# A hybrid decoder step on one core: the planner's attention in four parts, a new DMA price, and filler products where the plan leaves TensorE idle

## The chip, the core and the metric

The kernel runs on one core of a Trainium2 chip. The time is the device time of one execution in microseconds; of the kernel before there are three runs. One more execution was taken with the hardware profiler, and its rows are what this document reads.

## The reference

One inference step of a one-layer decoder in float32, for 512 prompt tokens and 8 sequences of 8 new tokens (64 sample tokens), so 576 columns in all. Every token goes through one combined input projection `w_in`; three branches read it, and their gated, normalized outputs go through `w_out`:

- a state-space branch (S5), with a scan over the tokens;
- latent attention (MLA): 8 heads; the query has a part of 128 and a rotary part of 64. `q = rmsnorm(concat(q_nope, rope(q_rot)))`, keys and values come from a latent of 256, the prompt attends causally over itself, each sample token over 1024 paged positions and the new ones;
- cross attention of 4 heads over 256 memory tokens, for prompt and sample.

```python
o = concat([rmsnorm(y_ssm) * silu(g_ssm), rmsnorm(y_mla) * silu(g_mla), rmsnorm(y_mem) * silu(g_mem)])
return x + o @ w_out
```

## The kernel before, in words

Activations stand transposed in SBUF: 128 features by 576 tokens, taken as two halves of 288 columns. Every float32 operand is split into a rounded high part and the rest (`split`, line 815), and a product is three TensorE products of those parts (`mm3`, line 845). Weights come in units of 128x512 (`wunit`, line 850): a load on SP's queue, then the high part on ScalarE or VectorE, then the low part on VectorE or, for the parts named in `ADDED` (line 32), by a DMA on GpSimd's queue that adds.

The order of the work isn't that of the code. `record` (line 2104) runs through the whole computation once and writes down every operation with the part that it belongs to: `x`, `u`, `e`, `q`, `gates0` to `gates3`, `memkv`, `mla` (attention of the prompt), `samp` (attention of the sample), `mems` (memory attention of the sample), `out` and so on. Then:

- `arrange` (line 369) gives every operation a key. A table, `ROWS` (line 41), has a row for each group of parts with two fractions of the plan's whole TensorE time, and a part's operations are spread between the two; no key is smaller than that of an operation that is waited for. From the keys come due times.
- `schedule` (line 428) plays the five engines through with costs of its own, and takes for each engine that is free the ready operation that is due first. An operation may be ahead of the oldest unfinished one by at most `self.window` (line 310; 57.7 us for TensorE, 40.7 us for SP). It also places the tiles in SBUF and in the eight PSUM banks. Prices of TensorE are by columns (line 720), with a model of the clock's two levels (`Clock`, line 265). A load on SP's queue costs 0.53 us of SP (line 601), and lands after 0.65 us, its bytes at 355e3 bytes a us, and 0.7 us more (lines 602 and 603).
- `emit` (line 648) issues the instructions in the order that came out. Each engine works through its own in that order, and waits on semaphores where an operand or a buffer isn't there yet.

The operations near the change:

- `consts` (line 921) sets `ones` (128x128) and a tile of zeros (128x288), and issues 16 products of the two (`WARM`) before the first real ones. The zeros' tile is free again after that.
- `mla_prompt` (line 1606) splits the query latent, and works in two halves of four heads. Each half begins with `mla_rot` (line 1444): 48 products for the rotary parts, the rotation on VectorE and GpSimd, and then 16 loads on SP's queue that move 32 rows each into another order (line 1469). `mla_group` (line 1477) follows twice, for two heads each: query products, sums of squares, key products with another round of norms (a row of them goes out to HBM and comes back spread over all partitions), values, and `mla_head` with its softmax.
- `mla_sample_q` (line 1620) begins with the query norms of all eight heads, so that `samp` can begin only when the last group of `mla` has its norms. `mems` needs nothing of `mla`.
- `out_proj` (line 2059) is the last product, 16 tiles of 96 products.

Of the kernel before, what the change touches and what calls it, by code (L numbers as in the profile page):

```python
# [18 lines left out]
P = 128  # L19
NT = 576  # L20
HF = 288
# [7 lines left out]
AFTER = ("mla", "samp")  # L29
SUMMED = (0, 1)  # L30
WHOLE = ("mla",)
ADDED = ("mla", "mems")
# [9 lines left out]
    (["x", "c", "u", "xn", "u3"], 0.0260741, 0.0604397),  # L42
    (["params"], 0.0288371, 0.0594688),
    (["e"], 0.054421, 0.13581),
    (["memkv"], 0.0589691, 0.14307),
    (["qm"], 0.113623, 0.153941),
    (["gates1"], 0.140543, 0.3),
    (["gates0"], 0.162105, 0.34697),
    (["scan"], 0.0965253, 0.273106),
    (["ssm", "glu"], 0.296516, 0.401341),  # L50
    (["memq", "memh"], 0.0899708, 0.278225),
    (["q", "kv", "kr"], 0.19873, 0.351389),
    (["gates2"], 0.322613, 0.380623),
    (["gates3"], 0.348796, 0.384288),
    (["mla"], 0.408448, 0.505007),
    (["samp"], 0.469029, 0.791363),
    (["mems"], 0.60639, 0.775131),
    (["fin0", "fin1", "fin2", "fins"], 0.649241, 0.728233),
    (["out"], 0.796155, 0.986057),
# [205 lines left out]
class Clock:  # L265
# [3 lines left out]
    def __init__(self):  # L269
        self.work, self.state, self.last = {}, {-1: 1.0, 0: 1.0}, 0  # L270
# [19 lines left out]
class Plan:  # L290


    def __init__(self, F, R, PS, sizes, place):
        self.F, self.R, self.PSt, self.sizes, self.place = F, R, PS, sizes, place
        self.ops = []
        self.tiles = []
        self.part = ""
        self.parts = {}
        self.lead = 0.0
        self.trace = None  # L300
        self.soon = 19.2555
        self.edf = True
        self.margin = [0, 0, 730, 0, 0, 0, 0]
        self.steal = 0.2575
        self.look, self.stall, self.tol = 15, 175.4667, 5.0000
        self.late = False
        self.hide = 0.6578
        self.early = 0.07
        self.slack = 1.0
        self.window = [57.6874, 40.6910, 40.6910, 40.6910, 40.0202]  # L310
# [58 lines left out]
    def arrange(self, rows):  # L369
# [21 lines left out]
        for o in reversed(self.ops):  # L391
            d = max(o.forms[o.eng][1], o.weights)
            if o.eng == SP:
                d = 2.5 + d / 355e3
            elif o.info == "dma_start":
                d = 5.9
            took[o.pos] = d
            k = key[o.pos]
            x = k if o.eng == PE else k + self.soon
            for s in o.succ:  # L400
                x = min(x, due[s.pos] - d - latency(o.eng, s.eng))
            due[o.pos] = x
# [25 lines left out]
    def schedule(self):  # L428
# [49 lines left out]
        dma_free = 0.0  # L478
# [13 lines left out]
        while len(order) < n:  # L492
# [18 lines left out]
            for e in range(5):  # L511
# [73 lines left out]
                for it in look:  # L585
                    heapq.heappush(h, it)
                if got is None:
# [12 lines left out]
                if e == SP:  # L600
                    avail[e] = now + (1.13 if op.info == "page" else 0.53)
                    dma_free = max(dma_free, avail[e] + 0.65) + dur / 355e3
                    op.end = dma_free + 0.7
                else:
# [5 lines left out]
                    if e == PE:  # L610
                        dur = clock.run(op.start, dur)
                    op.end = op.start + dur
# [152 lines left out]
class Hymba:  # L765
# [155 lines left out]
    def consts(self):  # L921
# [6 lines left out]
        self.G.memset(z.bitcast(F32), 0.0)  # L928
        for _ in range(WARM):
            self.mm(ps[:, :HF], self.ones, z, True, True)  # L930

# [674 lines left out]
    def mla_prompt(self):  # L1606
# [7 lines left out]
        for g in range(2):  # L1614
            qr, sq = self.mla_rot(g)
            for i in range(2):
                self.mla_group(2 * g + i, qr, sq)
# [460 lines left out]
    def run(self):  # L2078
        nc = self.nc
        with self.tc.tile_pool(name="sb", bufs=1) as sb, self.tc.tile_pool(name="pp", bufs=1, space=PSUM) as pp, \  # L2080
# [17 lines left out]
            self.record()  # L2098
            plan.arrange(ROWS)
# [74 lines left out]


# [12 lines left out]
```

## Time and profile before

| | before |
|---|---|
| median of 3 runs | 1185.97 us (1184.35 to 1188.2) |
| the profiled execution | 1190.08 us, span 1188.3 us |
| busy TensorE products | 1150.2 us, 97% of the span |
| busy VectorE | 849.0 us, 71% |
| busy ScalarE | 562.7 us, 47% |
| granted TensorE clock, mean | 0.993 |
| chain that ended last | TensorE 74%, VectorE 13%, DMA 7%, ScalarE 3% |

The span runs from the first instruction to the last one; 1.8 us of the profiled execution lie around it. A busy TensorE isn't yet one at its peak, since the ends of products are modelled: where two rows have the same busy time, their counts of products tell them apart. A granted clock of 1.00 is the higher of two levels, 2.4 GHz, and 0.50 the lower, 1.2 GHz.

### The profile page before, as it was taken

Reading aid. Unit: us, or ns where it says so; the run is one execution under the profiler, and the core shown is the slowest. Engines: PE = TensorE matmul, PEld = TensorE weight load, DVE = VectorE, ACT = ScalarE, POOL = GpSimd, SP = SyncE. Lnnn points to the kernel's source line nnn. Section 1 sums busy time; section 2 is a strip of 40 time slices with the busy share of each in tenths; the row PEclk is TensorE's granted clock in tenths of the full one; section 3 lists DMA queues with packets and bytes.
Section 4 is the critical chain, followed back from the end, with each engine's and each line's share of the span. In section 5 each row is a group of like instructions: output and inputs, shape, how many; then the busy total and the mean of one; then the engine's idle time right before and its main releaser. Section 6 shows DMA issues by size and latency. Waiting matters only on the chain.

```text
span 1188.3 us, 24276 instructions
## 1 busy us (share of the span) xinstructions
PE 1150.2 (97%) x8428; PEld 1097.8 (92%) x8428; DVE 849.0 (71%) x2252; ACT 562.7 (47%) x1712; POOL 201.3 (17%) x356
## 2 busy tenths in 40 slices
PE   8999999999999999998898999999999999999998
PEld 8989998999999999998786888899898899999998
DVE  7999599985697865457887987778999975322210
ACT  7446234431224433244764566666798863311200
POOL 1121012000114421012131210123453300000000
PEclk9999999999999999999998999999999998999999
DMA  9276211332313224467573331458778844634410
GB/s 328 91 213 213 73 62 58 125 130 78 118 45 101 94 75 149 147 192 178 148 196 97 89 94 43 120 156 206 203 186 242 213 140 132 201 111 132 146 48 30
DMA packets 98509, 160.51 MB, mean 135 GB/s; under 512 B 11378, under 2 KB 37362, under 8 KB 98386
## 3 DMA queue, kind: packets, MB, share of 16 engines
q1 hardware_dynamic: 90898, 145.33, 38.6%
q0 software_dynamic: 7488, 13.63, 6.5%
q8 instruction: 66, 1.08, 0.4%
q14 instruction: 57, 0.47, 0.1%
HBM read 125.20 MB, written 17.73 MB: 120 GB/s over the span
## 4 chain that ended last, share of the span: by engine, by line
PE 74%; DVE 13%; DMA 7%; ACT 3%; issue 2%; SPq 1%; POOL 0%; ACTq 0%; DVEq 0%
PE PS L680 72%; DVE t L680 9%; DVE F L680 4%; ACT t L680 3%; DMA t<-in_w_in 2%; PE PS L679 1%; DMA t<-re 1%; DMA t<-t 1%; SPq L680 1%; DMA t<-in_pages 1%; DMA t<-in_w_uk 1%; DMA t<-in_memT 0%; DMA t<-in_w_ukT 0%; ACT F L680 0%; DMA t<-in_cmv 0%
## 5 line engine op out<-in xcount | busy, mean ns | idle before, releaser
L680 PE MATMUL PS<-t,t 128*128 128x288 f32 (+7 forms) x8076 | 1133.1, 300 | 25.5 <-ACT t L680 17.5
L680 PEld LDWEIGHTS PS<-t,t 128*128 128x128 f32 (+2 forms) x8076 | 1067.8, 186 | 66.8 <-ACT t L680 22.0
L680 ACT ACTIVATE t<-t 128x512 fp32r<-128x512 f32 (+7 forms) x495 | 293.1, 620 | 375.3 <-DVE t L680 111.2
L680 DVE TENSOR_TENSOR t<-t,t 128x512 fp32r<-128x512 f32 (+12 forms) x616 | 354.2, 598 | 110.3 <-ACT t L680 62.5
L680 DVE TENSOR_TENSOR t<-PS,t 128x288 f32<-128x288 f32 (+5 forms) x226 | 90.9, 429 | 109.5 <-PE PS L680 105.0
L680 ACT ACTIVATE t<-PS 128x256 f32<-128x256 f32 (+7 forms) x246 | 86.6, 389 | 75.9 <-PE PS L680 43.2
L680 ACT ACTIVATE F<-PS 128x128 f32<-128x128 f32 (+1 forms) x264 | 71.4, 292 | 28.3 <-PE PS L680 25.0
L680 POOL TENSOR_TENSOR t<-t,t 128x384 fp32r<-128x384 f32 (+10 forms) x49 | 53.5, 1099 | 174.0 <-DVE t L680 119.4
L680 DVE TENSOR_SCALAR t<-t 128x512 fp32r<-128x512 f32 (+7 forms) x151 | 61.6, 419 | 29.2 <-PE PS L680 6.1
L680 POOL DMA_DIRECT2D t<-t x52 | 46.9, 908 | 150.6 <-ACT t L680 84.5
L680 DVE TENSOR_REDUCE F<-t 128x4 f32<-128x512 f32 (+1 forms) x73 | 51.7, 726 | 17.7 <-ACT t L680 17.5
L677 POOL MEMSET t<- 128x4 f32 (+2 forms) x100 | 33.5, 368 | 145.8 <-PE PS L680 107.7
L680 ACT ACTIVATE t<-t,F 128x576 fp32r<-128x576 f32 (+6 forms) x76 | 47.0, 632 | 20.0 <-DMA t<-t 11.9
L680 DVE SCALAR_TENSOR_TENSOR t<-t,t 128x576 f32<-128x576 f32 (+1 forms) x68 | 52.2, 769 | 4.6 <-ACT t L680 4.3
L680 ACT ACTIVATION_READ_ACCUMULATOR F<-PS 128x1 f32 x256 | 55.4, 219 | 0.0
L680 DVE SCALAR_TENSOR_TENSOR t<-t,F,t 128x576 fp32r<-128x576 f32 (+5 forms) x68 | 49.5, 735 | 8.1 <-ACT t L680 5.2
L680 ACT COPY t<-PS 128x64 f32<-128x64 f32 (+8 forms) x167 | 39.7, 287 | 23.2 <-PE PS L680 23.1
L680 DVE SCALAR_TENSOR_TENSOR F<-F 128x64 f32<-128x64 f32 (+5 forms) x157 | 35.1, 229 | 2.0 <-ACT F L680 0.6
L680 ACT ACTIVATE F<-F 128x256 f32<-128x256 f32 (+5 forms) x56 | 24.4, 435 | 21.8 <-DVE F L680 21.7
L680 DVE TENSOR_SCALAR t<-PS 128x256 fp32r<-128x256 f32 (+7 forms) x68 | 27.3, 408 | 9.8 <-PE PS L679 4.5
L679 PE MATMUL PS<-t,t 128*128 128x128 f32 (+1 forms) x152 | 29.6, 270 | 2.5 <-ACT t L680 1.7
L680 ACT ACTIVATE t<-PS,F 128x256 f32<-128x256 f32 (+4 forms) x39 | 18.5, 495 | 20.9 <-DVE F L680 9.6
(79 smaller groups left out, 425.5 us busy)
## 6 DMA issues: line engine op xcount, KB each, us to landing
t<-in_w_in SPq DMA_DIRECT2D x124, 256.0 KB, 3.2
t<-in_w_out SPq DMA_DIRECT2D x64, 256.0 KB, 4.6
t<-in_pages SPq DMA_DIRECT2D x64, 224.0 KB, 3.2
t<-t POOLq DMA_DIRECT2D x52, 256.0 KB, 4.4
t<-in_xT SPq DMA_DIRECT2D x32, 288.0 KB, 5.4
t<-re SPq DMA_DIRECT2D x32, 256.0 KB, 4.3
t<-in_pages SPq DMA_DIRECT2D x64, 128.0 KB, 2.3
re<-t SPq DMA_DIRECT2D x24, 256.0 KB, 2.1
```

What stands on the lines that cost most here:

```text
L677: return real(r["out"], r["value"])
L679: return real(r["out"], r["in_"], r["identity"])
L680: return real(**r)
```

## The change

It does six things.

1. The part `mla` is cut in five: `mla` keeps the latent's split and the loads of cosines and sines, `rot0` and `rot1` are the two calls of `mla_rot`, `mla0` and `mla1` the groups of the two halves. `rot1` gets a row of its own, ahead of the others.
2. All rows of the table get new numbers.
3. The planner prices loads anew, and lets at most eight be in flight.
4. Where TensorE finds no operation in the plan for more than `idle` = 0.5 us and a bank is free, `schedule` puts in a product of `ones` and zeros (128x128 by 128x288) into that bank, and goes on so until a real operation can start.
5. So that the zeros' tile lives to the end, a last product of `ones` and zeros stands at the end of `out`.
6. Some constants of the planner are rounded; `stall`, its weight for a weight load that isn't done, goes from 175 to 119.

```diff
-AFTER = ("mla", "samp")
+AFTER = ("mla0", "mla1", "samp")
-WHOLE = ("mla",)
-ADDED = ("mla", "mems")
+WHOLE = ("rot0", "rot1", "mla0", "mla1")
+ADDED = ("mla", "rot0", "rot1", "mla0", "mla1", "mems")
...
-    (["gates2"], 0.322613, 0.380623),
-    (["gates3"], 0.348796, 0.384288),
-    (["mla"], 0.408448, 0.505007),
-    (["samp"], 0.469029, 0.791363),
-    (["mems"], 0.60639, 0.775131),
-    (["fin0", "fin1", "fin2", "fins"], 0.649241, 0.728233),
-    (["out"], 0.796155, 0.986057),
+    (["gates2"], 0.3239, 0.4028),
+    (["gates3"], 0.3464, 0.3882),
+    (["rot1"], 0.3909, 0.3979),
+    (["mla", "rot0", "mla0", "mla1"], 0.4149, 0.5198),
+    (["samp"], 0.5183, 0.7914),
+    (["mems"], 0.5517, 0.7204),
+    (["fin0", "fin1", "fin2", "fins"], 0.6163, 0.729),
+    (["out"], 0.8, 1),
...
-        self.look, self.stall, self.tol = 15, 175.4667, 5.0000
+        self.look, self.stall, self.tol = 15, 119.4500, 5.0000
         self.late = False
+        self.filler, self.idle = None, 0.5
...
             if o.eng == SP:
-                d = 2.5 + d / 355e3
+                d = 3.3 + d / 400e3
...
+                if got is None and e == PE and self.filler and now > clock.busy + self.idle and order and free[BANKS] and front < n:
+
+                    op = self.filler(free[BANKS][-1][0])
+                    op.start, op.eng, op.dur = now, PE, clock.run(now, op.forms[PE][1])
+                    op.end = avail[PE] = now + op.dur
+                    order.append(op)
+                    progressed = True
+                    continue
...
                 if e == SP:
-                    avail[e] = now + (1.13 if op.info == "page" else 0.53)
-                    dma_free = max(dma_free, avail[e] + 0.65) + dur / 355e3
-                    op.end = dma_free + 0.7
+                    avail[e] = now + (1.13 if op.info == "page" else 0.5)
+                    dma_free = max(dma_free, avail[e] + 0.85) + dur / 400e3
+                    op.end = dma_free + 1.0
+
+                    flight.append(op.end)
+                    if len(flight) >= 8:
+                        avail[e] = max(avail[e], flight[-8])
...
                     if e == PE:
                         dur = clock.run(op.start, dur)
+                        clock.busy = op.start + dur
...
         for g in range(2):
+            self.plan.part = f"rot{g}"
             qr, sq = self.mla_rot(g)
+            self.plan.part = f"mla{g}"
             for i in range(2):
                 self.mla_group(2 * g + i, qr, sq)
...
         self.out_proj()
 
+        self.mm(self.bank()[:, :HF], self.ones, self.zero, True, True)
```

The function `filler` builds the product of `ones` and `self.zero` for a bank's address, without any operation that it waits for or that waits for it in the plan. The rows of the table that are left out change in the third or fourth decimal, with two exceptions: `params` begins at 0.0406 in place of 0.0288 and ends at 0.0666 in place of 0.0595, and `scan` ends at 0.2631 in place of 0.2731.

## Rows read from the trace of the kernel before

**Rows 1.** The page: span, products of TensorE, granted clock in 40 slices.

```profile
span 1188.3 us, 24276 instructions
...
PE 1150.2 (97%) x8428; PEld 1097.8 (92%) x8428; DVE 849.0 (71%) x2252; ACT 562.7 (47%) x1712; POOL 201.3 (17%) x356
...
PEclk9999999999999999999998999999999998999999
```

**Rows 2.** Windows of 30 us: busy time (count) by engine, granted clock, DMA share, GB/s.

```profile
540.00:570.00 30.00, 25.52 (x176) 22.58 (x175) 20.72 (x53) 14.81 (x35) 6.70 (x8) 1.00 0.71 164
570.00:600.00 30.00, 27.69 (x200) 24.87 (x198) 25.72 (x101) 20.97 (x56) 6.14 (x8) 1.00 0.64 166
600.00:630.00 30.00, 26.18 (x193) 23.91 (x192) 26.76 (x101) 20.81 (x53) 9.63 (x10) 1.00 0.59 166
630.00:660.00 30.00, 26.17 (x153) 22.42 (x152) 22.25 (x70) 12.09 (x31) 4.32 (x6) 0.83 0.55 146
...
690.00:720.00 30.00, 28.94 (x213) 26.98 (x213) 25.69 (x100) 16.64 (x72) 2.98 (x10) 1.00 0.22 67
...
1050.00:1080.00 30.00, 30.00 (x227) 30.00 (x227) 7.56 (x14) 6.38 (x11) 0.00 (x0) 1.00 0.39 122
```

**Rows 3.** Timeline of TensorE's products in the first 16 us: start, length, idle before.

```profile
1.27 4.21 PE L680 MATMUL PS<-R 128*128 128x288 f32 x16 [1.27 <-POOL R L677]
5.28 0.82 PE L680 MATMUL PS<-t,t 128*128 128x288 f32 x2
9.24 7.05 PE L680 MATMUL PS<-t,t 128*128 128x288 f32 x34 [3.14 <-ACT t L680]
```

**Rows 4.** Windows within the first 21 us, as in rows 2.

```profile
9.30:14.30 5.00, 5.00 (x21) 5.00 (x22) 5.00 (x9) 4.96 (x9) 0.00 (x0) 1.00 1.05 397
16.00:21.00 5.00, 5.00 (x40) 5.00 (x39) 5.00 (x9) 5.00 (x9) 0.00 (x0) 1.00 1.02 383
```

**Rows 5.** The chain that ended last, from 642 to 652 us.

```profile
642.63 3.46 DMA t<-t
...
646.21 0.96 DVE t L680 x2
...
647.96 3.90 PE PS L680 x14
```

**Rows 6.** Timeline of SP's loads in the prompt's attention; t<-t are the rotary ones.

```profile
555.30 12.22 SPq L680 DMA_DIRECT2D t<-t  x16
...
569.22 1.29 SPq L680 DMA_DIRECT2D t<-re  x3
...
638.25 4.97 SPq L680 DMA_DIRECT2D t<-t  x8
...
643.95 4.59 SPq L680 DMA_DIRECT2D t<-t  x6
```

**Rows 7.** Windows around the first fall of the clock, as in rows 2.

```profile
642.70:646.10 3.40, 1.60 (x11) 1.22 (x11) 0.92 (x2) 0.58 (x2) 0.18 (x1) 0.95 0.48 144
646.10:649.50 3.40, 1.54 (x3) 0.75 (x4) 3.11 (x7) 2.10 (x6) 0.00 (x0) 0.50 0.50 124
649.50:653.00 3.50, 3.50 (x20) 3.42 (x19) 1.69 (x5) 1.70 (x5) 0.00 (x0) 0.50 0.54 141
653.00:656.00 3.00, 3.00 (x12) 2.71 (x11) 1.72 (x8) 1.15 (x2) 0.88 (x1) 0.50 0.89 257
```

**Rows 8.** Windows around the second fall of the clock, as in rows 2.

```profile
986.40:990.50 4.10, 4.10 (x39) 4.09 (x37) 0.96 (x3) 0.02 (x1) 0.00 (x0) 1.00 0.85 268
990.50:997.30 6.80, 6.80 (x32) 6.66 (x31) 3.09 (x5) 2.68 (x6) 0.00 (x0) 0.50 0.24 72
997.30:1004.10 6.80, 6.80 (x53) 6.80 (x53) 4.31 (x21) 3.50 (x12) 0.00 (x0) 1.00 0.00 0
```

**Rows 9.** DMA issues: tensor, queue, count, KB each, median us to landing.

```profile
t<-in_w_in SPq DMA_DIRECT2D x124, 256.0 KB, 3.2
...
t<-re SPq DMA_DIRECT2D x32, 256.0 KB, 4.3
```

**Rows 10.** Waits of TensorE: us in total, times, longest.

```profile
PE PS L680 <- ACT t L680: 17.5, 13, 3.5
```

**Rows 11.** Timeline of TensorE: the first product that needs all heads' query norms.

```profile
684.29 1.12 PE L680 MATMUL PS<-t,R 64*128 64x512 f32 x2
```

More of the change, by code (lines that the diff above doesn't have):

```diff
@@ L41 @@
 ROWS = [[
[L42 to L52, printed above, removed]
-    (["gates2"], 0.322613, 0.380623),
-    (["gates3"], 0.348796, 0.384288),
-    (["mla"], 0.408448, 0.505007),
-    (["samp"], 0.469029, 0.791363),
-    (["mems"], 0.60639, 0.775131),
-    (["fin0", "fin1", "fin2", "fins"], 0.649241, 0.728233),
-    (["out"], 0.796155, 0.986057),
+    (["x", "c", "u", "xn", "u3"], 0.0262, 0.0602),
+    (["params"], 0.0406, 0.0666),
+    (["e"], 0.0556, 0.1349),
+    (["memkv"], 0.0573, 0.1431),
+    (["qm"], 0.1186, 0.1564),
+    (["gates1"], 0.1405, 0.3),
+    (["gates0"], 0.1591, 0.347),
+    (["scan"], 0.0927, 0.2631),
+    (["ssm", "glu"], 0.2928, 0.4021),
+    (["memq", "memh"], 0.09, 0.2678),
+    (["q", "kv", "kr"], 0.1967, 0.3521),
+    (["gates2"], 0.3239, 0.4028),
[6 more added lines that the diff above has]
+    (["out"], 0.8, 1),
 ]]
@@ L269, in __init__ @@
     def __init__(self):
-        self.work, self.state, self.last = {}, {-1: 1.0, 0: 1.0}, 0
+        self.work, self.state, self.last, self.busy = {}, {-1: 1.0, 0: 1.0}, 0, 0.0
     def at(self, t):
@@ L300, in __init__ @@
         self.trace = None
-        self.soon = 19.2555
+        self.soon = 19.2600
         self.edf = True
         self.margin = [0, 0, 730, 0, 0, 0, 0]
-        self.steal = 0.2575
-        self.look, self.stall, self.tol = 15, 175.4667, 5.0000
+        self.steal = 0.2600
+        self.look, self.stall, self.tol = 15, 119.4500, 5.0000
         self.late = False
-        self.hide = 0.6578
+        self.filler, self.idle = None, 0.5
+        self.hide = 0.6600
         self.early = 0.07
         self.slack = 1.0
-        self.window = [57.6874, 40.6910, 40.6910, 40.6910, 40.0202]
+        self.window = [57.6900, 40.6900, 40.6900, 40.6900, 40.0200]
     def sb(self, n, dt=F32, rows=P):
@@ L477, in schedule @@
         backfree, onfree = 0.0, False
-        dma_free = 0.0
+        dma_free, flight = 0.0, []
         clock = Clock()
@@ L491, in schedule @@
         now = 0.0
-        while len(order) < n:
+        while front < n:
             while releases and releases[0][0] <= now + 1e-9:
@@ L928, in consts, with filler @@
         self.G.memset(z.bitcast(F32), 0.0)
+        self.zero = z
         for _ in range(WARM):
             self.mm(ps[:, :HF], self.ones, z, True, True)
+    def filler(self, addr):
+        t = Tile_(512, BANKS)
+        t.addr = addr
+        ps = View(t, bass.AP(tensor=self.plan.PSt.tensor, offset=0, ap=[[self.plan.PSt.ap[0][0], P], [1, HF]]))
+        kw = dict(out=ps, lhsT=self.ones, rhs=self.zero, start=True, stop=True)
+        op = Op()
+        op.eng, op.forms, op.info, op.part, op.tiles, op.pred, op.succ = PE, {PE: self.T.form("matmul", kw)}, "filler", "filler", [], [], []
+        op.weights, op.half, op.key, op.done = 0.0, False, 0.0, True
+        return op
     def consts2(self):
@@ L2098, in run @@
             self.record()
+            plan.filler = self.filler
             plan.arrange(ROWS)
```

## The prediction

> **What bounds the kernel now.** First the page's line of engines: TensorE's products are busy for 1150.2 of 1188.3 us, and no other engine comes near [rows 1]. So the time is TensorE's products, plus 38.1 us in which none runs, plus what the products lose at the lower clock. The line of the granted clock shows two slices below 9; everything else is at 2.4 GHz. Then the windows of 30 us tell where the rest lies. The last stage runs 227 products per window with no idle time, which is the density to compare with. The prompt's attention has 176, 200, 193 and 153 products in its four windows, and 4.48, 2.31, 3.82 and 3.83 us of idle time, 14.4 in all, while VectorE is busy for at most 26.76 of 30 us and ScalarE for at most 20.97 [rows 2]. No engine is full there: the stage waits on chains of short steps. The change can gain in four places: the start, the attention's idle time, and the two falls of the clock.
>
> **1. The start.** The 16 constant products are over at 5.28 us, two real ones follow, then 3.14 us of nothing until a load's split is done [rows 3]. From 9.30 to 14.30 us TensorE makes 21 products of 288 columns in 5.00 us, 238 ns each; from 16 to 21 us it makes 40, with those cut by the edges [rows 4]. The clock's column says 1.00 in both, but a product of 288 columns in 238 ns is the 1.2 GHz level: the record of the clock isn't there yet, and the counts decide. The engine had stood idle before. Fillers go into just such a hole, since the plan too has to wait for the first loads there. If they keep the engine busy from 5.28 to 9.24 us, the 21 products may come at the higher clock: 21 x (238 - 132) = 2.2 us, with 132 ns from the 227 products per 30 us [rows 2]. The data keep up: x tiles and weights are split by VectorE and ScalarE, full in that window but for the same work that later feeds 40 products per 5 us [rows 4]. Bounds: 0 if the clock rises no earlier; -3.1 if the hole itself shrinks too, which fillers can't do. I take -2.3, counting the product that straddles the end.
>
> **2. The second half's rotary part, moved ahead.** At 644.5 us TensorE stops for 3.5 us. The chain that ended last names the cause: a rotary load lands after 3.46 us, two VectorE steps follow, and only then do the sums of squares at 647.96 go on [rows 5]. VectorE works in order, and behind its step on the late load stand the steps that those sums need. The load is late because 16 of its kind sit on SP's queue from 638.25 us on, 0.62 us of the queue each in the first eight and 0.77 in the next six [rows 6]. The pause then costs a second time: the clock falls at once, and the three windows after it are at 0.50 with 1.54 + 3.50 + 3.00 = 8.04 us of busy time [rows 7], half of which, 4.0 us, the higher clock would save. With `rot1` ahead of the first group, those 16 loads are long done by then. Bound of the gain: 3.5 + 4.0 = 7.5 us. What is late next: `rot0`'s own 16 loads held SP for 12.22 us, with the read-back of the key norms queued behind them until 569.22 [rows 6]; 16 more at that place take as long again. The cover is `rot1`'s 48 products, 48 x 0.132 = 6.3 us, and the gates that now end later. So 12.2 - 6.3 = 5.9 us could come back at worst; I take 1.5, since only the group's own loads stand behind the queue and the planner may now put them ahead of `rot1`'s. Term: -7.5 + 1.5 = -6.0, between -7.5 and -1.6.
>
> **3. The other rows and the price of loads.** The rest of the attention's idle time is 14.4 - 3.5 = 10.9 us [rows 2]. A better order could regain all of it, a worse one add as much; these are the bounds. A load of 256 KB (262144 bytes) was priced at 0.53 + 0.65 + 0.74 + 0.70 = 2.62 us and is now 0.50 + 0.85 + 0.66 + 1.00 = 3.01; the rows say 3.2 for weights and 4.3 for the read-back [rows 9]. So the new price closes 0.39 of a gap of 1.68 us, a quarter, for the load that is furthest off; a quarter of 10.9 is 2.5, and only some of these waits are for loads. I take -1.0. The Trainium skill ("DMA: Bandwidth & Descriptors", "Anatomy of one DMA", for descriptors written by software) gives 2.0 us and the bytes at 436e3 a us, 2.6 us by estimate, and by it the old price was right and this term is nothing; the rows above disagree with it, and I go by them.
>
> **4. The second fall, at 990.5 us.** It comes without any idle time: 4.10 of 4.10 us busy before it, 32 products in 6.80 us in it, 53 in the 6.80 after [rows 8]. Fillers go only where the plan finds no operation, and here it found one each time. 0, with a bound of -3.4 (half of 6.80) should the new order break up the small products.
>
> **5. What fillers cost.** Fillers stand in TensorE's own order; a real product that is ready earlier than planned stands behind them. TensorE waited 13 times for ScalarE's tiles, 17.5 us in all [rows 10]; a filler too many at each is 13 x 0.132 = 1.7 us, and none at all is 0. I take 1.0. A filler also waits for its bank's last reader on ScalarE or VectorE; the next real product mostly waits for the same engine, so nothing is added. The product at the end adds 0.13, and the zeros' 128x288 in SBUF nothing as long as plans fit.
>
> **Sum:** -2.3 - 6.0 - 1.0 + 0 + 1.0 + 0.1 = -8.2 us. The profiled execution took 1190.08 us, 4.1 more than the median: 1181.9 beside 1190.1, so 1177.8 beside 1185.97. I say 1178.
>
> **Rivals.**
> - *The wait moves and doesn't go.* The SP queue is as long as before, only earlier, and what `rot0` and `rot1` hold up at the attention's head is worth what was gained at 644 us (5.9 back, and a pause that lowers the clock there as it did here). For it: 12.22 us of queue, already with a read-back behind [rows 6]. Against it: the gates still have products at that place. Then only the start is left: -2.3 + 1.1, about 1185.
> - *Slower: the sample's attention comes too late to fill in.* From 684.29 us on, its products are mixed with the last groups' [rows 11], and there the idle time is 1.06 us per 30, against 3.8 before [rows 2]. The change moves `samp` from 0.469 to 0.518, 57 us on TensorE's 1150.2 [rows 1]. If its loads and splits are asked for so much later that the attention's last 45 us run alone, that costs 45/30 x (3.8 - 1.1) = 4.1 us, and one more pause that drops the clock, 4.0; with no gain from term 2, since the second half is then bound by its own chains: -2.3 + 8.1 + 1.1 = +6.9, 1193. It decides once the sample's first product comes later than the attention's last. Against it: those first products need the last group's norms in either plan.
> - *Fillers overrun.* The plan counts 0.13 us for one, but 16 constants took 5.28 - 1.27 us at the start, 0.25 each [rows 3]: there they last twice as long as planned. From 16 fillers on they reach past 9.24 us. With 27 (a planned hole of 4 us less 0.5) the first real products are 27 x 0.25 - 3.5 = 3.3 us late, which outweighs the gain of 2.3; with two fillers too many at 13 waits, 3.4, and no gain elsewhere, +4 to +5 before the new order's gains, some +2.5 with a part of them: 1188.5. The Trainium skill ("TensorE: Matmul & The Clock Gate", "Step-by-step: what each phase is for") says that TensorE keeps its products in program order and pulls only weight loads ahead, so nothing would overtake a filler; no row of before can show that.
>
> **How the numbers follow.** The forecast has 0.52; the wait that moves 0.18; the late sample 0.22; the overrun 0.08. The order of the whole kernel is drawn anew, and the idle time of the attention can go either way, hence the 0.22. A measurement of this kernel can tell about 0.3%, 3.6 us, from no change. The forecast's own range is 1168 to 1182.4, all faster; the second and fourth case are within 0.3%; the third is slower. Range: 1167 to 1195, which leaves out the tail of term 3's bound and the worst of the late sample.
>
> **What would show it.** Right: 21 early products at 132 ns; SP's 32 rotary loads in one block before the first group's, and none near the second half; no clock of 0.50 in the attention; 190 products or more in each window of 30 us there; the fall near the end still there. Wrong: idle time at the attention's head as long as the 3.5 us that left; a stretch after the attention's last product before the sample's first; fillers directly ahead of products whose operands had long been there.

## The result, and the profile after

The changed kernel takes 1174.74 us (median of 4 runs, 1174.41 to 1177.06) where the kernel before took 1187.09 in the same rounds (4 runs, 1184.35 to 1189.17): a ratio of 0.9899 [0.9875, 0.9924], 12.4 us faster. The forecast was 1178, 8 us faster, with a range of 1167 to 1195. So direction and range hold, and a third of the gain was not foreseen. Most of what follows is about which step it came from, since the total came out for other reasons than the sum's.

| | before | after |
|---|---|---|
| the profiled execution | 1190.08 us, span 1188.3 | 1177.06 us, span 1175.3 |
| busy TensorE products | 1150.2 us | 1150.7 us |
| span less that | 38.1 us | 24.6 us |
| granted clock, mean | 0.993 | 0.992 |

First the page of the changed kernel: span, engines and granted clock in 40 slices.

```profile
span 1175.3 us, 24339 instructions
...
PE 1150.7 (98%) x8463; PEld 1099.9 (94%) x8463; DVE 848.5 (72%) x2242; ACT 562.4 (48%) x1722; POOL 198.4 (17%) x356
...
PEclk9999999999999999999999999999999998999999
```

Against [rows 1], TensorE has 35 more products, and its busy time is the same; the span is 13.0 us shorter, and time without a product fell by 13.5. The mean clock has not risen. So in these two profiles the gain shows as time without a product. The 35 added products last some 5 us by estimate (eleven push the first real one from 5.28 to 7.51 us, 24 more take 0.13 each), so the others must have become shorter by about as much, in part at the start (below). Where the idle time lay, the windows of 30 us tell for the attention (columns as in [rows 2]):

```profile
540.00:570.00 30.00, 25.43 (x178) 22.91 (x177) 23.48 (x56) 17.03 (x40) 7.98 (x10) 1.00 0.65 167
570.00:600.00 30.00, 28.89 (x208) 25.78 (x207) 26.23 (x101) 20.81 (x59) 4.66 (x7) 1.00 0.49 126
600.00:630.00 30.00, 29.22 (x209) 25.55 (x208) 24.91 (x102) 18.86 (x51) 4.24 (x6) 1.00 0.45 110
630.00:660.00 30.00, 29.43 (x211) 26.06 (x209) 25.14 (x100) 19.19 (x56) 4.79 (x6) 1.00 0.42 120
690.00:720.00 30.00, 29.00 (x188) 27.09 (x187) 22.68 (x67) 19.10 (x88) 10.02 (x28) 0.89 0.58 146
```

The attention's four windows have 4.57, 1.11, 0.78 and 0.57 us of idle time, 7.0 in all where there were 14.4, and 806 products where there were 722. That is 7.4 of the 13.5 us. The clock no longer falls there. It falls elsewhere, at 690 to 720 us, where [rows 2] had 213 products and 1.00.

The start, as TensorE's timeline (start, length, idle before):

```profile
1.28 6.40 PE L695 MATMUL PS<-R 128*128 128x288 f32 x27 [1.28 <-POOL R L692]
7.51 0.42 PE L695 MATMUL PS<-t,t 128*128 128x288 f32 x2
```

and as a window with the columns of [rows 4]:

```profile
9.30:14.30 5.00, 5.00 (x39) 5.00 (x39) 4.76 (x8) 5.00 (x10) 0.00 (x0) 1.00 1.04 388
```

Eleven fillers stand behind the 16 constants, and are over at 7.51 us, before the data are there (0.95 us of idle time remain, where [rows 3] had 3.14: 2.2 more of the 13.5). From 9.30 to 14.30 us TensorE makes 39 products in place of 21 [rows 4].

SP's rotary loads, and what TensorE waited for on ScalarE in the whole span (us in total, times, longest):

```profile
548.11 17.48 SPq L695 DMA_DIRECT2D t<-t  x24
...
566.27 4.95 SPq L695 DMA_DIRECT2D t<-t  x8
```

```profile
PE PS L695 <- ACT t L695: 5.0, 9, 1.7
...
PE PS L694 <- ACT t L695: 2.8, 4, 1.6
```

All 32 loads are issued from 548 to 571 us, and none near the second half. [Rows 6] had 16 at 555 and the other 16 from 638 on. The row of [rows 10] shrank from 17.5 us in 13 waits to 5.0 in 9; the second row above, of another line of the kernel, is not in [rows 10] and had 2.0 us in 4 before.

Last the clock, in windows with columns as in [rows 7], around the two falls that this profile has:

```profile
693.00:699.90 6.90, 6.58 (x58) 6.40 (x57) 6.82 (x15) 2.84 (x15) 2.01 (x10) 1.00 0.32 111
699.90:706.70 6.80, 6.12 (x23) 5.48 (x22) 5.32 (x31) 5.60 (x25) 4.04 (x14) 0.50 0.61 171
...
970.00:976.40 6.40, 6.40 (x59) 6.40 (x57) 1.99 (x5) 0.86 (x3) 0.00 (x0) 1.00 0.81 258
976.40:986.60 10.20, 10.02 (x43) 9.68 (x43) 4.85 (x14) 2.92 (x8) 0.00 (x0) 0.50 0.01 2
986.60:996.80 10.20, 10.20 (x78) 10.20 (x77) 6.66 (x21) 4.62 (x13) 0.00 (x0) 1.00 0.36 106
```

The fall at 645.8 us [rows 7] is gone, a new one of 6.8 us has come at 699.9, and the one near the end [rows 8] now lasts 10.2 us in place of 6.8. The recorded time at 1.2 GHz is the same 17.0 us, in other places. The record of the clock begins where the clock first rises, at 14.3 us before and at 7.0 us after; what lies ahead of that counts as full speed.

### The profile page after: what moved, and what is told of

Same layout as the page of the kernel before. It is cut to its first block, busy times and chain, and to the rows that moved or that the text cites. A ratio compares the mean times of both kernels' runs of the same rounds, so it can differ in the third digit from the quotient of the medians.

```text
span 1175.3 us, 24339 instructions
## 1 busy us (share of the span) xinstructions
PE 1150.7 (98%) x8463; PEld 1099.9 (94%) x8463; DVE 848.5 (72%) x2242; ACT 562.4 (48%) x1722; POOL 198.4 (17%) x356
## 4 chain that ended last, share of the span: by engine, by line
PE 49%; DVE 5%; ACT 3%; DMA 2%; SPq 2%; issue 1%; POOL 0%; ACTq 0%; DVEq 0%; POOLq 0%
PE PS L695 49%; DVE t L695 3%; ACT t L695 2%; DVE F L695 2%; DMA t<-in_pages 1%; SPq L695 1%; DMA t<-in_w_uv 1%; PE PS L694 1%; SPq L1708 0%; ACT F L695 0%; DMA t<-in_w_uk 0%; SPq L1709 0%; DMA re<-t 0%; DVE PS L695 0%; POOL t L695 0%
## 5 line engine op out<-in xcount | busy, mean ns | idle before, releaser
L695 PE MATMUL PS<-t,t 128*128 128x288 f32 (+9 forms) x8076 | 1126.1, 299 | 9.9 <-ACT t L695 5.0
L695 ACT ACTIVATE t<-t 128x512 fp32r<-128x512 f32 (+7 forms) x486 | 286.5, 620 | 374.7 <-PE PS L695 121.4
L695 DVE TENSOR_TENSOR t<-t,t 128x512 fp32r<-128x512 f32 (+12 forms) x620 | 361.9, 607 | 125.8 <-ACT t L695 67.1
L695 DVE TENSOR_TENSOR t<-PS,t 128x288 f32<-128x288 f32 (+6 forms) x226 | 89.8, 428 | 89.8 <-PE PS L695 82.6
L695 ACT ACTIVATE t<-PS 128x256 f32<-128x256 f32 (+6 forms) x253 | 87.7, 392 | 66.2 <-PE PS L695 32.6
L695 POOL TENSOR_TENSOR t<-t,t 128x256 f32<-128x256 f32 (+10 forms) x45 | 41.4, 929 | 192.0 <-DVE t L695 72.7
L695 ACT ACTIVATE t<-t,F 128x576 fp32r<-128x576 f32 (+6 forms) x80 | 49.5, 633 | 14.4 <-DMA t<-t 8.2
L694 PE MATMUL PS<-t,t 128*128 128x128 f32 (+1 forms) x152 | 26.1, 269 | 5.8 <-ACT t L695 2.8
L695 DVE TENSOR_SCALAR t<-PS 128x256 fp32r<-128x256 f32 (+8 forms) x61 | 24.0, 403 | 9.9 <-PE PS L695 5.4
L695 POOL TENSOR_SCALAR t<-t 64x64 f32<-64x64 f32 (+4 forms) x24 | 21.9, 911 | 33.3 <-DVE t L695 32.0
```

The costliest lines, as they stand in the source:

```text
L694: return real(r["out"], r["in_"], r["identity"])
L695: return real(**r)
```

## The experiments

Twelve runs, four at a time; each four ran on one chip and share the runs of the kernel before. "Clock" is the mean of the granted clock over the runs of a kernel. "At full clock" is the median times that clock. It is an estimate of what would be left if all that the lower clock costs were given back; it holds as far as TensorE bounds the kernel, and is only used to tell a gain in order from a gain in clock. Since a low start counts as full in some executions and not in others, differences of 0.001 to 0.002 in the clock tell little. A ratio is taken to the runs of before on the same chip, whose median went from 1184.18 to 1187.97 us, so between chips medians and ratios can differ.

| kernel | median us | ratio to before | clock | at full clock |
|---|---|---|---|---|
| before (first four) | 1184.18 | | 0.9915 | 1174.2 |
| new order, no fillers | 1181.96 | 1.0002 [0.9973, 1.0031] | 0.9874 | 1167.1 |
| new order, fillers at the start only | 1180.59 | 0.9973 [0.9949, 0.9997] | 0.9874 | 1165.7 |
| changed, `rot1` back | 1177.53 | 0.9954 [0.9929, 0.998] | 0.9939 | 1170.4 |
| before, `rot1` ahead | 1182.54 | 0.9999 [0.9973, 1.0024] | 0.9908 | 1171.6 |
| before (second four) | 1185.85 | | 0.9905 | 1174.6 |
| changed | 1176.67 | 0.9921 [0.9895, 0.9947] | 0.9912 | 1166.3 |
| before, with fillers | 1185.63 | 0.9996 [0.9972, 1.0019] | 0.9899 | 1173.7 |
| before, ten more constants | 1187.14 | 1.0002 [0.998, 1.0025] | 0.9886 | 1173.6 |
| changed, constants among products of 64 columns | 1175.43 | 0.9917 [0.989, 0.9944] | 0.9977 | 1172.7 |
| before (third four) | 1187.97 | | 0.9899 | 1176.0 |
| new order, no fillers (again) | 1184.41 | 0.9981 [0.9965, 0.9997] | 0.9860 | 1167.8 |
| new order, late fillers only | 1179.20 | 0.9936 [0.9913, 0.9959] | 0.9895 | 1166.8 |
| changed, fewer such constants, and some in `e` | 1179.40 | 0.9941 [0.992, 0.9961] | 0.9932 | 1171.3 |
| changed | 1175.81 | 0.9908 [0.9889, 0.9928] | 0.9908 | 1165.0 |

The changed kernel was timed three times in all: 0.9899, 0.9921, 0.9908. Single runs of the kernel before went from 1177.1 to 1192.5 us, and so small differences are read with care.

### The order without its fillers

The same order of instructions to the letter, with all 34 fillers left out; run twice.

```diff
         for op in self.order:
+            if op.info == "filler":
+                continue
```

> The changed kernel's order to the letter, with its 34 planned fillers left out as the instructions are issued (the last constant product at the end stays). Nothing depends on a filler, so only their own time and the clock change. Theory A (fillers are worth the start alone): the clock is low until about 14 us again, 21 products at 238 ns, +2.5 us; the 22 fillers near 404 and 872 us stand directly ahead of products that go on without a pause, and leaving them out gives back up to 1.5 + 1.4 = 2.9 us. Sum 1174 to 1177, no change beyond 0.3%. Theory C (fillers hold the clock later too): new stretches at 0.50 near 404 and 872 us, each of 7 to 10 us, 3.4 to 5 us each: 1180 or more.

Measured: 1.0002 [0.9973, 1.0031]. And again on another chip:

> The changed kernel's order without its planned fillers once more, now on the same chip as the changed kernel. Theory D (order and fillers only help together): 0.997 to 1.002 of the kernel before, as the first time, with the changed kernel near 0.991. Theory E (the new order is the gain and the first measure of this kernel was a chip's own): 0.992 to 0.996.

Measured: 0.9981 [0.9965, 0.9997], where the changed kernel beside it had 0.9908 [0.9889, 0.9928]. **Without its fillers the new order is worth 0 to 0.2%.** That isn't for want of a better order: the span less the busy products is 31.4 us in the second profile (1181.7 - 1150.3) against 38.1 before, and at full clock the two runs give 1167.1 and 1167.8, 7 to 8 us below their own before. But the mean clock is 0.9874 and 0.9860, some 0.004 lower than before's, which is 5 us. What the order gained, the clock took back. The profile of the second run shows one of the places, where ten fillers and two more would stand. TensorE's timeline of it:

```profile
405.89 0.79 PE L697 MATMUL PS<-t,t 128*128 128x288 f32 x4 [0.46 <-ACT t L697]
408.08 1.33 PE L697 MATMUL PS<-t,t 128*128 128x288 f32 x4 [1.40 <-DVE t L697]
```

Its windows (the 400.00 one holds the pauses, the next one the clock behind them):

```profile
400.00:407.90 7.90, 6.03 (x43) 5.28 (x42) 7.87 (x15) 3.69 (x8) 5.06 (x7) 1.00 0.49 160
407.90:411.30 3.40, 3.22 (x30) 3.15 (x31) 2.93 (x6) 0.00 (x0) 0.00 (x0) 0.50 0.00 0
```

And the changed kernel at the same place, TensorE's timeline (PS<-R are the fillers):

```profile
403.91 0.43 PE L695 MATMUL PS<-R 128*128 128x288 f32 x2
404.53 0.80 PE L695 MATMUL PS<-t,t 128*128 128x288 f32 x4 [0.19 <-ACT t L695]
405.17 1.48 PE L695 MATMUL PS<-R 128*128 128x288 f32 x10
406.73 1.10 PE L695 MATMUL PS<-t,t 128*128 128x288 f32 x8
```

and its windows:

```profile
400.00:407.90 7.90, 7.63 (x62) 7.08 (x61) 7.80 (x16) 2.34 (x6) 3.80 (x5) 1.00 0.44 141
407.90:411.30 3.40, 3.40 (x57) 3.40 (x55) 2.82 (x8) 0.63 (x1) 0.53 (x1) 1.00 0.17 57
```

Where the fillers are left out TensorE idles for 0.46 and 1.40 us, and the clock falls right behind; where they stand, 57 products pass in those 3.40 us in place of 30. Set side by side by the number of the real product, the kernel without loses 1.4 us from 404 to 411 us. It isn't so in each execution: the profile of the first run has the same two pauses (0.46 and 1.37 us) and no fall behind them, and loses nothing there.

```profile
407.90:411.30 3.40, 3.40 (x60) 3.40 (x59) 2.85 (x7) 0.63 (x1) 0.53 (x1) 1.00 0.12 39
```

That profile has a fall of 3.4 us at 875.9 instead, right behind a pause of 1.64 us where the other ten late fillers would stand. The second run's has one more at 568, where no filler stands in either kernel:

```profile
568.30:571.70 3.40, 2.77 (x8) 1.90 (x9) 2.84 (x7) 2.42 (x7) 0.00 (x0) 0.51 0.62 167
```

Of the three profiles of this order without the late fillers (these two, and the one with fillers at the start only) two have falls near 407 and 568 us and one near 876; none of the six profiles of this order with them has any of the three.

### Which fillers

The 11 at the start alone, and the 23 later ones alone, by the time that the plan gives them:

```diff
+            if op.info == "filler" and op.start > 10.0:
+                continue
```

> The changed kernel's order to the letter, with only the 11 fillers of the first 10 us issued. Theory A: the clock is up at 7 us as in the changed kernel, the 22 later fillers were pure cost, so 1.5 to 2.9 us less than the changed kernel: about 1172. Theory C: the clock falls near 404 or 872 us: 1178 or more.

Measured: 0.9973 [0.9949, 0.9997], with the clock at 0.9874 as without any filler.

```diff
+            if op.info == "filler" and op.start < 10.0:
+                continue
```

> The changed kernel's order, with the 22 fillers near 404 and 872 us and the last product, but without the 11 at the start. Theory D with the gain at the start: 0.996 to 0.999 of before. With the gain in the later ones (the clock held at 404 and 872 us, some 1.5 us each, as the falls of the two kernels without them suggest): 0.993 to 0.996. Between the two, each place has its share.

Measured: 0.9936 [0.9913, 0.9959], beside 0.9981 [0.9965, 0.9997] with none and 0.9908 [0.9889, 0.9928] with all on the same chip. **The late fillers are worth 0.45%**, 5.2 us, and the intervals don't overlap; the same comparison with those at the start in place, 0.9973 against the changed kernel's 0.9899 to 0.9921, says 0.5 to 0.7%, across chips. The clock went from 0.9860 to 0.9895, 4.1 us of the 5.2. The direct saving at 404 us is 1.4 of the 5.2 in the profile that has the fall there; the rest is spread over other places, and isn't the same in two profiles. The start's fillers are worth 0.29% both times (1.0002 to 0.9973, 0.9936 to 0.9908), but both pairs of intervals overlap, so that is less sure.

### The fillers on the order of before

The planner of before with the fillers alone (28 of them, and the last product; table, parts and prices untouched):

```diff
+                if got is None and e == PE and self.filler and now > clock.busy + self.idle and order and free[BANKS] and front < n:
+                    op = self.filler(free[BANKS][-1][0])
...
+        self.mm(self.bank()[:, :HF], self.ones, self.zero, True, True)
```

> The kernel before, with its own table, parts and prices, and the fillers of the change (with the last constant product): 28 fillers, 10 of them at the start and the others late in the sample's attention. Theory A (fillers are worth the start): -2.3 + 1, 0.998 to 1.000 of before. Theory C (fillers are most of the change's gain): 0.990 to 0.994.

Measured: 0.9996 [0.9972, 1.0019]. Nothing, though the span less the busy products fell to 29.1 us (1183.7 - 1154.6), and the start had 40 products in 9.30 to 14.30 us there too. Its later fillers stand near 761, 893 and 928 us, where the profile of before has no fall of the clock, and a fall near 645 and one near 987 us are still in its own. And the start by itself, ten more constants behind the 16:

```diff
+            if op.eng == PE and op.part == "x":
+                warm += 1
+                if warm == WARM:
+                    for _ in range(10):
+                        op.forms[PE][0]()
```

> The kernel before, its order to the letter, with ten more constant products issued directly behind the 16 that open it, and nothing else. It measures the start alone. Theory A: clock up before 9.3 us, 21 products at 132 in place of 238 ns, 2.2 us, 0.998 of before. Theory C: the same; the rest of its gain would then have to be in the later fillers.

Measured: 1.0002 [0.998, 1.0025]. Its windows at the start and at 70 us:

```profile
9.30:14.30 5.00, 5.00 (x40) 5.00 (x39) 5.00 (x9) 4.99 (x9) 0.00 (x0) 1.00 1.02 382
...
70.00:74.00 4.00, 1.64 (x9) 1.09 (x8) 3.94 (x11) 2.69 (x5) 0.78 (x1) 0.99 0.91 250
74.00:84.20 10.20, 9.95 (x48) 9.82 (x48) 8.28 (x24) 5.25 (x21) 4.35 (x8) 0.50 0.51 165
```

The same windows of the kernel before:

```profile
70.00:74.00 4.00, 4.00 (x26) 3.49 (x24) 4.00 (x21) 0.44 (x1) 0.00 (x0) 1.00 0.93 267
74.00:84.20 10.20, 7.90 (x58) 6.61 (x56) 9.59 (x29) 6.87 (x26) 2.94 (x5) 1.00 0.69 203
```

From 50 to 70 us this kernel is 4.3 us ahead, product by product. At 70 us TensorE is busy for 1.64 of 4.00 us, waiting for what isn't there yet, and the clock falls for 10.2 us. At 90 us it is 0.3 us ahead. **In this profile what the start gained was given back at the next place where the data were late**, by way of the clock. The profile of before with fillers has no fall there, and its time didn't drop either, so this is one way and not the only one.

### The rotary part of the second half

The changed kernel with `rot1` back between the halves, planned anew (24 fillers):

```diff
-    (["rot1"], 0.3909, 0.3979),
-    (["mla", "rot0", "mla0", "mla1"], 0.4149, 0.5198),
+    (["mla", "rot0", "mla0", "rot1", "mla1"], 0.4149, 0.5198),
```

> The changed kernel with the row of rot1 taken away and rot1 put back between mla0 and mla1 in their own row; fillers, prices and all other rows stay. The plan is drawn anew from the attention on. Theory A (rot1 ahead is worth some 6 us): a pause of 2 to 4 us with SP's queue full of rotary loads before the second half, perhaps with a fall of the clock: 1179 to 1182. Theory B (rows and prices did it, rot1 is nothing): 1173 to 1177.

Measured: 0.9954 [0.9929, 0.998]. SP's rotary loads of the second half in its timeline:

```profile
630.30 8.67 SPq L694 DMA_DIRECT2D t<-t  x13
```

TensorE's timeline, the first products behind the rotary part:

```profile
638.81 2.24 PE L694 MATMUL PS<-t,t 128*72 128x384 f32 x12 [0.73 <-ACT t L694]
```

And the sum over the attention's four windows, from 540 to 660 us:

```profile
sum 120.00, PE 112.94 PEld 98.47 DVE 98.99 ACT 72.41 POOL 21.79; mean PE 28.24 PEld 24.62 DVE 24.75 ACT 18.10 POOL 5.45
```

The pause of 3.5 us is 0.73 here, and the idle time of the attention is 120 - 112.94 = 7.1 us, as in the changed kernel with `rot1` ahead. So what else changed in the planner, numbers and prices, takes the pause away without the move.

The move alone, on the table of before (parts cut in five, no new prices, no fillers):

```diff
-    (["mla"], 0.408448, 0.505007),
+    (["rot1"], 0.3909, 0.3979),
+    (["mla", "rot0", "mla0", "mla1"], 0.408448, 0.505007),
```

> The kernel before with the parts cut as in the change and rot1 in a row of its own ahead of the attention; the attention's other rows, the prices and everything else are those of before, no fillers. Theory A: the pause at 644 us and the fall of the clock behind it are gone, 6 to 7.5 us less than before, 1179.5 to 1181. Theory B: within 3 us of before, since what rot1 gains is lost where the 32 rotary loads now stand on SP's queue.

Measured: 0.9999 [0.9973, 1.0024]. SP's timeline at the attention's head:

```profile
547.02 23.74 SPq L681 DMA_DIRECT2D t<-t  x32
```

TensorE's timeline there:

```profile
566.17 5.92 PE L681 MATMUL PS<-t,t 128*72 128x384 f32 x33 [4.93 <-ACT t L681]
```

And the window behind the pause:

```profile
566.20:569.60 3.40, 3.40 (x11) 2.62 (x12) 2.85 (x10) 1.76 (x5) 0.00 (x0) 0.53 0.46 114
```

Much of the rival "the wait moves and doesn't go" is here: all 32 loads in one block of 23.74 us, a pause of 4.93 us at the head in place of 3.5 in the middle, and the clock falls behind it there (11 products in 3.40 us). But the head had a pause before the move too, of 2.27 us,

```profile
565.54 2.29 PE L680 MATMUL PS<-t,t 128*72 128x384 f32 x12 [2.27 <-ACT t L680]
```

and the attention's four windows, with a stretch behind them, read in the kernel with the move:

```profile
sum 120.00, PE 109.87 PEld 96.85 DVE 98.32 ACT 72.63 POOL 22.18; mean PE 27.47 PEld 24.21 DVE 24.58 ACT 18.16 POOL 5.55
...
685.40:692.20 6.80, 6.80 (x32) 6.34 (x32) 5.37 (x35) 2.55 (x13) 1.98 (x8) 0.50 0.11 34
```

The attention's idle time is 120 - 109.87 = 10.1 us, where before had 14.4. So not all of the wait came back at the head. The profile has a fall of 6.8 us at 685.4 that the one of before has not, but one profile of each doesn't show where the gain went. The ratio leaves room for a gain of 3.2 us at most, and "at full clock" the move shows 2.6.

### The falls of the clock without idle time

In the changed kernel both falls come while TensorE is busy (6.58 of 6.90 and 6.40 of 6.40 us ahead of them). Its products by form from 970 to 976.4 us (count, busy us, mean ns, idle before):

```profile
L695 PE MATMUL PS<-t,t 128*128 128x64 f32 x44 | 5.2, 277 | 0.0
```

44 of the 59 have 64 columns, the thin ones below; they start every 0.11 us (the 277 ns are from start to end, and they overlap), and TensorE's weight loads are busy throughout (6.40 of 6.40 us in the window shown of after). To test that they make the clock fall, one constant product of 288 columns was put behind every third of them (27, by the 8490 products of its profile beside 8463; the expectation counts 33):

```diff
+            if op.eng == PE and op.info != "filler":
+                thin = thin + 1 if 2.5 * op.forms[PE][1] < op.weights else 0
+                if thin >= 3 and op.spare is not None:
+                    self.filler(op.spare).forms[PE][0]()
+                    thin = 0
```

> The changed kernel's order to the letter, and in addition a constant product behind every third of the products in a row that are bound by their weight load (64 columns; some 27 of 33 lie in the two runs of such products near 697 and 974 us in the changed kernel's profile). Theory: the clock falls there (6.8 and 10.2 us at 0.50) because the array does little although the engine is never idle. If so, both stretches are gone: -3.4 - 5.1 + 33 x 0.12 = -4.5 us, 0.996 of the changed kernel. Rival: the clock doesn't follow the columns, the falls stay, and the 33 products add 4 us.

Measured: 0.9917 [0.989, 0.9944], beside 0.9921 [0.9895, 0.9947] for the changed kernel on the same chip. Its windows at the two places:

```profile
699.90:706.70 6.80, 6.00 (x40) 5.26 (x39) 5.17 (x30) 5.60 (x27) 3.80 (x13) 1.00 0.60 141
...
976.40:986.60 10.20, 9.00 (x68) 8.62 (x68) 6.54 (x25) 4.37 (x15) 0.00 (x0) 1.00 0.01 3
```

Both falls are gone, and the mean clock is 0.9977, with 0.997 or more in each of its six runs, where none of the changed kernel's on that chip is over 0.993. All seven profiles of this order without such constants have both falls. So **the stretches of thin products are the cause of these two falls**; whether it is their few columns or the weight load that each has was not told apart. But no time was gained that can be told. The constants (PS<-R) and the thin products in the timeline:

```profile
697.28 0.38 PE L702 MATMUL PS<-R 128*128 128x288 f32 x1
697.49 0.41 PE L702 MATMUL PS<-t,t 128*128 128x64 f32 x3
697.74 0.38 PE L702 MATMUL PS<-R 128*128 128x288 f32 x1
```

Each constant adds what it lasts, some 0.14 us (a constant and three thin products start every 0.47 us, three alone take 0.33): 27 x 0.14 = 3.8 us, against the 7.7 us that the clock gave back (10.4 - 2.7, by the table's clocks). At full clock the kernel became 6.4 us longer; 2.6 of these have no row.

Fewer (17, behind every fifth), and 12 constants more ahead of the first and the fifth product of `e`, where some profiles show a fall at 83 us (the entry for the 13th issued none, by the profile):

```diff
+            if op.eng == PE and op.part == "e":
+                for _ in range({0: 8, 4: 4, 12: 4}.get(e, 0) if spare is not None else 0):
+                    self.filler(spare).forms[PE][0]()
+                e += 1
...
+                if thin >= 5 and op.spare is not None:
```

> The changed kernel's order with two kinds of constant products added: one behind every fifth of the weight-bound products of 64 columns (17 in all, against 33 behind every third before), and 8 + 4 in the pauses near 79 and 81 us, ahead of the first and the fifth product of part e. Theory: the clock falls at 83 us (6.8 us in most profiles of this order), near 699 and near 974 us are gone; 17 x 0.12 = 2.0 us paid, 1.3 + 2.4 + 4.6 saved (the steps of the aligned profiles): -5 to -6 us, 0.995 of the changed kernel. Rival: a product in five isn't enough for the clock, and the pauses at 79 us are shorter than 12 products: within 0.2% of the changed kernel.

Measured: 0.9941 [0.992, 0.9961], by the medians 3.6 us slower than the changed kernel beside it (0.9908 [0.9889, 0.9928]; the intervals just overlap), with a clock of 0.9932 against 0.9908. Its profile has the last fall still, at full length:

```profile
976.00:986.20 10.20, 10.02 (x43) 9.68 (x42) 4.51 (x14) 2.92 (x8) 0.00 (x0) 0.50 0.01 2
```

There is one of 3.4 us at 699.5 too; none is at 83 us, but one of three profiles of the changed kernel has none there either. So the first half of the recorded rival holds: one constant in five isn't enough at 976 us. The hope of a kernel better than both fell here: the clock rose a little, and by the medians the constants cost more than it brought.

### The changed kernel again

Unedited, once in the second four and once in the third, as the measure for the others.

> The changed kernel itself, once more, so that the other runs have it on the same chip. Both theories: 0.988 to 0.993 of the kernel before, as measured first. If it is nearer to 0.997, then the three variants of it measured so far (no fillers 1.0002, start fillers 0.9973, rot1 back 0.9954) differ from it by less than they seem to.

> The changed kernel once more, as the measure for the three others on this chip: 0.989 to 0.993 of the kernel before.

Measured: 0.9921 [0.9895, 0.9947] and 0.9908 [0.9889, 0.9928]. Its three profiles have spans of 1175.3, 1172.7 and 1176.1 us for the same instructions.

## Why the prediction was right or wrong

**1. The start (-2.3): the mechanism is right, the sum is not.** 39 products came in the window where there were 21, at 128 ns each, and the clock was at 2.4 GHz from 7.0 us on. But the 21 were those of one profile. The same window without fillers at the start, in the second run without any:

```profile
9.30:14.30 5.00, 5.00 (x30) 5.00 (x30) 5.00 (x8) 5.00 (x9) 0.00 (x0) 0.73 1.05 404
```

and in the run with the late ones only:

```profile
9.30:14.30 5.00, 5.00 (x40) 5.00 (x39) 5.00 (x8) 4.54 (x9) 0.00 (x0) 1.00 1.04 388
```

So the clock can be up there without a filler, and 2.2 us is near the most that it had to give. And a time gained at the start counts only if nothing later is bound by something else. The extra constants on the order of before were 4.3 us ahead at 70 us and 0.3 at 90, and neither they nor the fillers moved its time. In the new order the start's fillers show 0.29%, 3.4 us, at the edge of what can be told. The step that failed is one that the sum takes without saying so, that a microsecond saved at the start is one saved at the end: a wait between 70 and 84 us was in the trace (7.90 of 10.20 us busy) and was not looked for.

**2. `rot1` moved ahead (-6.0): failed as put.** The reading of [rows 5 to 7] holds: late rotary loads, the pause, the fall of the clock; and in the changed kernel pause and fall are gone: 107 products in 642 to 656 us, as the row shows.

```profile
642.00:656.00 14.00, 14.00 (x107) 13.34 (x106) 13.45 (x63) 10.95 (x34) 1.47 (x2) 1.00 0.46 146
```

But the move isn't needed for that. Alone it gave 0.9999, with a pause of 4.93 us at the head; and with `rot1` left between the halves the rest of the change cut the pause to 0.73 us. In the changed kernel the move may still be worth something: with `rot1` back the ratio is 0.9954 [0.9929, 0.998] against 0.9899, 0.9921 and 0.9908 with it ahead. Only the second one's interval overlaps, but none of them is known to be of the same chip, the medians (1177.53 against 1174.74 to 1176.67) are 0.9 to 2.8 us apart, and the plan with `rot1` back has no fillers at 872 us. It isn't the pause, and no row was found for it, so this worth is not shown. The step that failed is "with `rot1` ahead of the first group, those 16 loads are long done", taken as what the move does to the time: alone, it made the other wait at the head longer. The 1.5 us taken back was the mis-sized number of the move alone; the worst case of 5.9, which leaves 1.6, is within what that run allows.

**3. Other rows and the price of loads (-1.0): far too small.** The attention's idle time fell by 7.4 us (14.4 to 7.0), and as much with `rot1` in either place; at full clock the new order without any filler is 7 to 8 us shorter than before. The step that failed is the "quarter of 10.9": it let the new prices speak for the rows too, whose own effect was left at nothing. Which part of the change saves it was not tried apart: numbers of the table (`memq` and `memh` too end 0.0104 earlier), prices of loads, the limit of eight in flight, or `stall`. On the prices, the profile of the changed kernel has, as DMA issues (count, KB each, median us to landing):

```profile
t<-in_w_in SPq DMA_DIRECT2D x124, 256.0 KB, 3.6
...
t<-re SPq DMA_DIRECT2D x32, 256.0 KB, 4.0
```

The new price of 3.01 us is still below both, as it was below [rows 9]. The Trainium skill ("DMA: Bandwidth & Descriptors", "Anatomy of one DMA") would have 2.6 us by estimate for such a transfer when its descriptors are written by software; these rows, of SP's queue, don't agree with it as a price here.

**4. The second fall (0): it stayed**, 10.2 us long in place of 6.8, and a like one came at 700 us. That fillers can't reach it was right: no idle time is there. The bound of -3.4 was not earned by small products broken up either: doing so ended both falls, and gained no time that can be told. The Trainium skill ("TensorE: Matmul & The Clock Gate", "HAM oscillation — how this bites in real kernels") puts the falls of the clock in a matrix product of few rows (thin M) down to waits for a DMA between groups of products; here TensorE was busy for 6.40 of 6.40 us ahead of the fall, with no wait, and the measurement decides.

**5. What fillers cost (+1.0): wrong in sign.** The term priced only what a filler can delay. The 23 late ones gain 5.2 us. They stood in real idle time (0.46 and 1.40 us at 406 us), so they delayed nothing: the real products behind them start at 404.53 and 406.73 us beside 405.89 and 408.08 without fillers, 1.36 and 1.35 earlier, and those ahead of the pauses were 1.36 earlier already. And the clock fell less: 0.9860 to 0.9895, 4.1 us of the gain. The Trainium skill's rule that products stay in program order ("TensorE: Matmul & The Clock Gate", "Step-by-step: what each phase is for") agrees with the thin ones of the experiments: there was no idle time around those, and each cost the 0.14 us that it lasts.

**The rivals.** The wait that moves was seen in part, and on the table of before alone. The late sample did not come: its first product stands where it stood [rows 11], a microsecond earlier, and TensorE is busy for 29.00 of 30 us at 690 to 720, with the clock as the change there.

```profile
683.20 1.10 PE L695 MATMUL PS<-t,R 64*128 64x512 f32 x2
```

The overrun did not come: 11 fillers in place of the 27 feared, over at 7.51 us with the data at 8.89.

**The signs.** Most of those named as right came: the early products at 128 ns, no rotary load near the second half, no clock of 0.50 in the attention, the last fall still there, and 190 products in three of the four windows (the first has 178, and 4.57 us of idle time beside 4.48). But the profile with `rot1` back shows all of them except the place of the loads, so they could not tell whether the move or the rest of the change was at work.

**The sum, as the runs have it.** By the medians of the third four, 1187.97, 1184.41, 1179.20 and 1175.81: the new order -3.6 (some -8 at equal clock, and +5 by its own loss of clock), the late fillers -5.2, those at the start -3.4, less sure; 12.2 in all. The forecast of -8.2 came near by luck: terms 1 and 2 gave nothing that can be told when each was tried alone on the order of before, and stood in for two that were left out, the new rows and the late fillers.

**What stays open.** Why the fillers at the start seem to count in the new order and not in the old one: some profiles of the changed kernel have a fall of 6.8 us at 83 us and the one above has none, and with or without these fillers the kernels are then within 1.4 us of each other at 110 us. Why the clock of the new order without the late fillers falls at 568 us, where they don't stand. And which of numbers and prices shortens the new order.

## What to carry to other kernels

A better order can lose in the clock what it gains in idle time, so time a new order by its median and its mean clock together, and put cheap constant products into idle time that is really there; into work without idle time they cost what they last. A microsecond saved early is only worth something if no later wait is for data that come at their own time: look for the next place where the engine waits before counting it. And of a step that is moved, ask what the new place has queued already: with 32 loads in one block, TensorE's pause was 4.93 us where the longest had been 3.5.

## What was not expected of the hardware

- The granted clock falls behind runs of products of 64 columns, though TensorE has no idle time (6.40 of 6.40 us busy, then 43 products in 10.20 us in place of 78). One product of 288 columns behind every third of them kept it up; behind every fifth, the fall of 10.2 us stayed.
- The clock of the same instructions doesn't fall at all the same places from run to run: of three profiles of the changed kernel two have a fall at 83 us and one has none there, and their spans differ by 3.4 us. Single runs of the kernel before differ by 15 us, and so one profile's falls are a sample and no property of the kernel.
